# Where the norm factors of two-tile weight granules are applied, and on which engine their high parts are made

## The chip, the cores and the metric

The kernel runs on one core of one Trainium2 chip. The metric is the device time of one execution in microseconds (us). Engines are named as in the profile: PE is TensorE, DVE VectorE, ACT ScalarE, POOL GpSimd, SP the engine that issues the transfers (SPq its DMA queue). PEld is PE's loading of weights, which overlaps its matmuls.

## What is computed

A stack of four blocks over a sequence of 1024 positions, model width 1024, in float32. The first block (chunked gating and dilated attention) and the projections before the SSD are not touched. What the change meets, cut from the reference:

```python
def rmsnorm_2(x, g):
    return rms(x) * g

# mamba2_mixer: state-space scan (SSD) over chunks of 128, 4 groups
acum = cumsum(dt_k * Ag, axis=1)
decay = exp(where(causal, acum[:, None] - acum[None, :], -inf))
y = ssd_chunked_scan(xs, dt, A, Bm, Cm) + d_skip * xs
y = rms(y * silu(z), in 4 groups) * y_g          # y_g: 2048 factors
h = h + y @ w_out                                # m_out: 2048 x 1024

# per_layer_embedding, after each of the two mixers
h = h + (p_i @ w_proj) * sigmoid(rmsnorm_2(h, norm_g) @ w_gate)   # ple_gate: 1024 x 1024

# stick_breaking_mixer: 16 heads, causal, weights from suffix sums of log(1 - sigmoid)
h = h + (o * silu(gate)) @ w_out                 # s_out: 1024 x 1024
```

A norm's factors `g` are not multiplied into the activations: row k of the weight matrix is multiplied by `g[k]` when the weight is prepared.

## The kernel before, in words

**Parts.** Each float32 matmul is made of three products of a shorter format: a value is split into a high part (a rounded copy) and a low part (the value minus the high part), and PE adds high x high, high x low and low x high. So each weight passes through a preparation before PE can use it.

**Granules.** Class `Weights` (lines 366 to 427) prepares weights in granules of up to 1024 columns per partition. `loads` issues a DMA into a raw slot (names `m0f`, `m208f`; up to three slots of 4 KB per partition). `splits` takes a split slot (`m8r`, `m16r`, `m24r`, `m192r`, `m200r`; later `m140r`) and makes the parts: with a norm factor, first a pass of POOL over the whole raw granule that multiplies by the factors (`Gtt`, line 508, `m0f<-m0f,cols`; `cols` holds the factors, a column for each k-tile); then the high part on ACT (`A`, line 485, `m8r<-m0f`), or on POOL where `hi_on_pool` is set (`Gts`, line 512); then the low part on POOL (`Gtt`, line 508, `m8r<-m0f,m8r`). After this the raw slot is free for the next load. A granule holds 8 k-tiles of 128 columns (kind "b") or 2 k-tiles of 512 (kinds "a" and "c"). Of the second kind with a factor there are 32: 16 of `m_out` (gain `ynorm`) and 8 in each of the two `ple_gate` matrices.

**Order.** Every engine runs its instructions in an order that is fixed when the program is written out. Class `Sched` (lines 245 to 306) sets it: streams (Python generators with a priority) yield what they wait for, an estimate of engine times says when that is ready, and whenever PE's estimated time comes to a stream whose wait is over, the one of the best priority goes on. A stream may have a slack: it then goes on that much later than its wait says (`SLACK` is 1200 ns). So a cost or a wait that changes in one place can change the order of everything behind it.

**Stages**, in the order of time: first block to about 1250 us; `mamba` (projections of z, x, B, C and dt; a depthwise convolution; the SSD); `mamba_out` (`m_out`, from some 1930 us on, whose first half starts while the SSD's last group still runs); the first `ple`; `stick` (attention, 2300 to 2950 us; `W.limit(2, 1)` leaves two split slots and one raw slot, and `hi_on_pool` is set in its gate at the last head pair); `stick_out` (`s_out` in two blocks `so0` and `so1`, then the second `ple`).

*In `mamba`* `ev` starts the stream `tables` when the last piece of dt is there (line 1577). It makes the cumulative sums `acum` (PE: `psum<-m172f 32x128` and `128x256`), stores and reloads them, and makes the decay tables (DVE: `m172f<-m172f,m92f 128x128`, 8, and `m92f<-m92f 128x128`, 16). On DVE it shares the order with the taps of the convolution (`m60f`, `m76f`, `m44f`), from which come the B and C of the SSD's first product (PE: `psum<-m76f,m60f`). The SSD itself uses `m92f` (a table loaded from `acum`), `m172f` and `m192f` on DVE and POOL.

*In `stick_out`* the stream `more` (lines 2155 to 2157) waits until all scores are done (`all_scored`) and gives six split slots; three raw slots (`W.all_raw`) come back after `so1`. `load_halves` and its `one` load pairs `stk` and `sgd`, multiply them on POOL and split the product (POOL, then DVE) into the `so` matmuls' left operand (`m92r`, the last of them). `embed` loads `p` through `m172f`.

Helpers: all ACT operations of this kind have line 485, DVE 489 to 500 (500 is the operation with two tensors and a scalar), POOL 508 (two tensors) and 512 (one), DMA 516, matmuls 523, transposes 534.

## Time and profile before

| | us |
|---|---|
| median of 3 runs | 3232.16 |
| fastest and slowest of them | 3229.4, 3235.44 |
| the profiled execution | 3230.68 |
| its span in the trace | 3228.9 |
| PE busy | 3065.7 (95% of the span) |
| DVE busy | 1670.1 (52%) |
| ACT busy | 1386.8 (43%) |
| POOL busy | 1268.7 (39%) |

The span runs from the first to the last instruction of the trace; the execution's time has 1.8 us more around it. Busy shares are means over stages with different limits. A wait of PE is put down to the instruction whose result came last. The granted clock (PEclk) is a fraction of PE's full 2.4 GHz; 0.50 is 1.2 GHz.

### The profile page before, as it was taken

Reading aid. Unit: us, or ns where it says so; the run is one execution under the profiler, and the core shown is the slowest. Engines: PE = TensorE matmul, PEld = TensorE weight load, DVE = VectorE, ACT = ScalarE, POOL = GpSimd, SP = SyncE. Lnnn points to the kernel's source line nnn. Section 1 sums busy time; section 2 is a strip of 40 time slices with the busy share of each in tenths; the row PEclk is TensorE's granted clock in tenths of the full one; section 3 lists DMA queues with packets and bytes.
Section 4 is the critical chain, followed back from the end, with each engine's and each line's share of the span. In section 5 each row is a group of like instructions: output and inputs, shape, how many; then the busy total and the mean of one; then the engine's idle time right before and its main releaser. Section 6 shows DMA issues by size and latency. Waiting matters only on the chain. (4 is left out here: it accounts for less than half of the span.)

```text
span 3228.9 us, 40412 instructions
## 1 busy us (share of the span) xinstructions
PE 3065.7 (95%) x15374; PEld 2556.2 (79%) x15374; DVE 1670.1 (52%) x2944; ACT 1386.8 (43%) x2465; POOL 1268.7 (39%) x772
## 2 busy tenths in 40 slices
PE   8999999999999999999999999899999999988989
PEld 6888888888888788887777777678887777876777
DVE  2111146666674421557576765432457777777542
ACT  4322155556564311433243323222457776765321
POOL 3233111111111432324464554552445565657551
PEclk9999999999999999999999999999999999999999
DMA  4112221121122853332333444450301111113521
GB/s 142 55 65 73 91 64 52 59 67 53 55 63 76 276 172 137 110 90 66 100 102 102 102 117 140 147 189 27 101 12 34 46 34 39 40 40 114 206 89 52
DMA packets 270549, 290.85 MB, mean 90 GB/s; under 512 B 14660, under 2 KB 202228, under 8 KB 270356
## 3 DMA queue, kind: packets, MB, share of 16 engines
q1 hardware_dynamic: 270356, 288.29, 28.7%
q8 instruction: 120, 1.97, 0.3%
q14 instruction: 73, 0.60, 0.1%
HBM read 216.80 MB, written 71.43 MB: 89 GB/s over the span
## 5 line engine op out<-in xcount | busy, mean ns | idle before, releaser
L489 DVE TENSOR_TENSOR m156r<-psum,m156r 128x384 fp32r<-128x384 f32 (+2 forms) x376 | 223.4, 605 | 146.7 <-ACT m156r L485 144.7
L485 ACT ACTIVATE m156r<-psum 128x384 fp32r<-128x384 f32 (+2 forms) x376 | 194.6, 533 | 202.8 <-PE psum L534 191.0
L508 POOL TENSOR_TENSOR m172f<-m172f,m24f 128x127 f32<-128x127 f32 (+7 forms) x128 | 188.4, 1483 | 143.5 <-DVE m24f L2045 103.7
L508 POOL TENSOR_TENSOR m8r<-m0f,m8r 128x1024 fp32r<-128x1024 f32 x46 | 112.8, 2451 | 295.1 <-ACT m8r L485 290.3
L508 POOL TENSOR_TENSOR m16r<-m0f,m16r 128x1024 fp32r<-128x1024 f32 (+1 forms) x47 | 119.9, 2551 | 271.7 <-ACT m16r L485 221.6
L534 PE MATMUL psum<-ident,m172f 128*128 128x128 f32 (+1 forms) x1314 | 206.2, 281 | 19.6 <-POOL m172f L508 7.6
L2045 DVE TENSOR_TENSOR_SCAN m24f<-m24f,zero 128x128 f32<-128x128 f32 (+7 forms) x128 | 206.8, 1630 | 7.1 <-ACT m24f L485 6.7
L485 ACT ACTIVATE m192f<-psum 64x256 f32<-64x256 f32 (+2 forms) x231 | 102.8, 446 | 243.6 <-PE psum L523 136.3
L534 PEld LDWEIGHTS psum<-ident,m172f 128*128 128x128 f32 (+1 forms) x1314 | 158.9, 144 | 45.6 <-POOL m172f L508 10.2
L508 POOL TENSOR_TENSOR smalls<-smalls,mhalf 128x1 f32<-128x1 f32 (+1 forms) x104 | 91.0, 875 | 218.5 <-DVE smalls L496 217.9
L523 PE MATMUL psum<-m200r,m108r 128*128 128x512 f32 (+1 forms) x480 | 150.1, 393 | 6.5 <-POOL m200r L508 3.3
L508 POOL TENSOR_TENSOR m24r<-m0f,m24r 128x1024 fp32r<-128x1024 f32 (+1 forms) x40 | 100.9, 2524 | 135.5 <-ACT m24r L485 135.1
L523 PE MATMUL psum<-m108r 128*128 128x512 f32 (+3 forms) x384 | 142.8, 374 | 3.1 <-DVE smalls L1414 1.6
L494 DVE TENSOR_SCALAR m172f<-m172f,smalls 128x512 f32<-128x512 f32 (+7 forms) x160 | 130.5, 816 | 27.4 <-POOL smalls L508 22.8
L500 DVE SCALAR_TENSOR_TENSOR m172f<-m172f,psum 128x512 f32<-128x512 f32 x64 | 43.7, 686 | 188.2 <-ACT m172f L485 144.1
L1414 DVE CUSTOM_DVE_ANT_0 m172f<-psum,m24f 128x512 f32<-128x512 f32 (+1 forms) x192 | 102.8, 553 | 65.1 <-PE psum L523 64.9
L1422 ACT ACTIVATE m172f<-m172f,smalls 128x128 f32<-128x128 f32 (+7 forms) x128 | 99.4, 776 | 82.8 <-DVE smalls L496 81.2
L523 PE MATMUL psum<-m44r,m8r 128*128 128x512 f32 x504 | 133.8, 400 | 1.1 <-DVE m108r L500 1.1
L523 PE MATMUL psum<-m76r,m8r 128*128 128x512 f32 x504 | 132.7, 397 | 0.0
L523 PE MATMUL psum<-m60r,m8r 128*128 128x512 f32 x504 | 132.6, 397 | 0.0
L523 PE MATMUL psum<-m44r,m16r 128*128 128x512 f32 x492 | 132.4, 406 | 0.0
L523 PE MATMUL psum<-m60r,m16r 128*128 128x512 f32 x492 | 130.5, 398 | 0.0
(413 smaller groups left out, 7758.8 us busy)
## 6 DMA issues: line engine op xcount, KB each, us to landing
m0f<-in_w_in_dram SPq DMA_DIRECT2D x48, 512.0 KB, 3.8
m0f<-in_m_in_dram SPq DMA_DIRECT2D x26, 512.0 KB, 4.0
m208f<-in_w_in_dram SPq DMA_DIRECT2D x24, 512.0 KB, 4.1
m92f<-acum SPq DMA_DIRECT2D x21, 512.0 KB, 9.1
m24f<-in_alibi_dram SPq DMA_DIRECT2D x16, 512.0 KB, 4.2
m172f<-zd SPq DMA_DIRECT2D x32, 256.0 KB, 10.1
yd<-m172f SPq DMA_DIRECT2D x32, 256.0 KB, 2.6
m108f<-hd SPq DMA_DIRECT2D x16, 512.0 KB, 5.9
```

The source lines that it names most:

```text
L485: self.nc.scalar.activation(out, in_, func, **k)
L489: self.nc.vector.tensor_tensor(out, a, b, op=op)
L494: self.nc.vector.tensor_scalar(out, a, s1, None, op0=op0)
L500: self.nc.vector.scalar_tensor_tensor(out, a, s, b, op0=op0, op1=op1)
L508: self.nc.gpsimd.tensor_tensor(out, a, b, op=op)
L523: self.nc.tensor.matmul(out, l, r, start=start, stop=stop)
L534: self.nc.tensor.transpose(out, in_, self.ident[:in_.shape[0], :in_.shape[0]])
L1414: nc.vector.tensor_tensor_reduce(row[:, k0:k0 + w], bank[:, :w], Tt[:, off + k0:off + k0 + w], 1.0, -3e38, op0=ALU.add, op1=ALU.max, accum ...
L1422: nc.scalar.activation(row[:, :n], row[:, :n], AF.Exp, bias=nm, accum_out=l)
L2045: nc.vector.tensor_tensor_scan(x[:, ::-1], x[:, ::-1], self.zero.to_broadcast([P, n]), 1.0, op0=ALU.mult, op1=ALU.add)
```

## The change

Granules with a factor and at most two k-tiles take a new branch of `splits`. Each k-tile's high part is made by ACT straight from the raw granule, with the factor column as the activation's scale; each low part by one operation of DVE, raw x factor - high part. POOL has no part in them, and the raw slot is free after the last DVE operation. Stream `tables` gets a slack of four times `SLACK`. Stream `more` also ends `hi_on_pool` and gives the three raw slots back, at `all_scored`; the line that gave them back after `so1` goes.

```diff
--- before.py
+++ after.py
@@ -403,6 +403,19 @@
             hi = g.out[:, :n].rearrange("p (k c) -> p k c", k=g.nk)
             lo = g.out[:, KB4:KB4 + n].rearrange("p (k c) -> p k c", k=g.nk)
             dep = g.loaded.t
+            if g.gain is not None and g.nk <= 2:
+
+                yield (dep, b.s.FA)
+                for k in range(g.nk):
+                    e = b.A(R(hi[:, k, :]), g.rawv[:, k, :], AF.Copy, dep, scale=g.gain[:, k:k + 1])
+                for k in range(g.nk):
+                    yield (e, b.s.FV)
+                    t = b.Vstt(R(lo[:, k, :]), g.rawv[:, k, :], g.gain[:, k:k + 1], hi[:, k, :], ALU.mult, ALU.subtract, e)
+                self.raw.put(g.slot, t)
+                g.hi, g.lo = R(hi), R(lo)
+                g.ready.t = t
+                yield 0.0
+                continue
             if g.gain is not None:
                 yield b.s.FG
                 dep = b.Gtt(g.rawv, g.rawv, g.gain.unsqueeze(2).to_broadcast([P, g.nk, g.nc]), ALU.mult, dep)
@@ -1574,7 +1587,7 @@
                 if ps.free_size() > n:
                     r = self.Vtt(dtx[:, t * 32:t * 32 + 32], ps[:, 256:], kc[:, 0:32], ALU.add, max(e, ke))
                     if t == NT - 1:
-                        s.spawn(1, tables(r))
+                        s.spawn(1, tables(r), 4 * SLACK)
                 e = self.A(o, ps[:, :n], AF.Tanh, e, scale=0.5)
                 e = self.Vstt(o, o, 1.0, ps[:, :n], ALU.add, ALU.mult, e)
                 s.spawn(4, store(cb, t, o, e))
@@ -2154,6 +2167,8 @@
 
         def more():
             yield self.all_scored
+            self.hi_on_pool = False
+            W.raw.slots = W.all_raw
             W.split.slots = W.all[:4] + [self.region(o, 8, "r") for o in (140, 148)]
 
         s.spawn(1, more())
@@ -2188,7 +2203,6 @@
 
         yield from self.gemm_a(act, self.J["so", 1], ev, fin, 4, begin, (5, 6, 7))
         W.split.slots = W.split.slots + W.all[4:]
-        W.raw.slots = W.all_raw
 
         def store(t, e):
             yield e
```

Three places in the order of the engines follow. Line numbers of the changed kernel are 11 to 14 higher, so its helpers stand at L498 (ACT), L502 to L513 (DVE), L521 and L525 (POOL), L529 (DMA), L536 and L547 (PE).

PE at the tables of `mamba`, where `m108r`, `m140r` and `m156r` are the normed activations, `m8r` and `m200r` the weights of a projection, and `m172f` the operand of the cumulative sums. Before:

```order
L523 MATMUL psum<-m156r,m8r 128x512 x12
L523 MATMUL psum<-m108r,m200r 128x512 x3
L523 MATMUL psum<-m172f 32x128 x8
L523 MATMUL psum<-m172f 128x256 x2
L523 MATMUL psum<-m108r,m200r 128x512 x9
L523 MATMUL psum<-m140r,m200r 128x512 x12
```

and now:

```order
L536 MATMUL psum<-m156r,m8r 128x512 x6
L536 MATMUL psum<-m172f 32x128 x8
L536 MATMUL psum<-m172f 128x256 x2
L536 MATMUL psum<-m156r,m8r 128x512 x6
L536 MATMUL psum<-m108r,m200r 128x512 x12
L536 MATMUL psum<-m140r,m200r 128x512 x12
```

The cumulative sums stand 9 matmuls sooner.

POOL where the first granules of `m_out` are prepared, among the SSD's operations (`m92f`, `m172f`, `m192f`, and `m208f<-m208f,cols`, which is a granule again). Before:

```order
L508 TENSOR_TENSOR m0f<-m0f,cols 128x1024
L508 TENSOR_TENSOR m92f<-m92f,m192f 128x1024
L508 TENSOR_TENSOR smalls<-smalls,mhalf 128x1
L508 TENSOR_TENSOR m200r<-m0f,m200r 128x1024
L508 TENSOR_TENSOR m208f<-m208f,cols 128x1024
L508 TENSOR_TENSOR m172f<-m172f,m92f 128x512
L508 TENSOR_TENSOR m24r<-m208f,m24r 128x1024
L508 TENSOR_TENSOR m0f<-m0f,cols 128x1024
L508 TENSOR_TENSOR m192f<-m208f,m192f 128x512
L508 TENSOR_TENSOR m172f<-m172f 128x512
L508 TENSOR_TENSOR m172f<-m172f,m92f 128x512
L508 TENSOR_TENSOR m24r<-m0f,m24r 128x1024
```

and what DVE has there now (L513 with `cols` is the new form; `x2` is one granule; `m40f` belongs to the last convolution's inputs, `m44f` to its taps):

```order
L502 TENSOR_TENSOR m172f<-m172f 128x512
L513 SCALAR_TENSOR_TENSOR m40f<-m40f,psum 128x512
L507 TENSOR_SCALAR m172f<-m172f,smalls 128x512
L509 TENSOR_SCALAR smalls<-smalls 128x1
L513 SCALAR_TENSOR_TENSOR m200r<-m208f,cols,m200r 128x512 x2
L513 SCALAR_TENSOR_TENSOR m24r<-m0f,cols,m24r 128x512 x2
L507 TENSOR_SCALAR m172f<-m172f,smalls 128x512
L513 SCALAR_TENSOR_TENSOR m44f<-m92f,m192f,m44f 128x1023
L513 SCALAR_TENSOR_TENSOR m24r<-m208f,cols,m24r 128x512 x2
L513 SCALAR_TENSOR_TENSOR m44f<-m92f,m192f,m44f 128x1022
L513 SCALAR_TENSOR_TENSOR m16r<-m0f,cols,m16r 128x512 x2
```

The granules' two or three passes of POOL are gone from its queue, and their pairs stand in DVE's, among evacuations, the SSD's scales and the taps.

POOL in the last stage, where the granules of `ple_gate` in the second ple are prepared (`m140r`, `m24r`, `m200r`; `smalls` is the norm's power function). Before:

```order
L508 TENSOR_TENSOR m0f<-m0f,cols 128x1024
L512 TENSOR_SCALAR m140r<-m0f 128x1024
L508 TENSOR_TENSOR smalls<-smalls,mhalf 128x1
L508 TENSOR_TENSOR m140r<-m0f,m140r 128x1024
L508 TENSOR_TENSOR smalls<-smalls,mhalf 128x1
L508 TENSOR_TENSOR m0f<-m0f,cols 128x1024
L512 TENSOR_SCALAR m24r<-m0f 128x1024
L508 TENSOR_TENSOR m24r<-m0f,m24r 128x1024
L512 TENSOR_SCALAR m200r<-m208f 128x1024
L508 TENSOR_TENSOR smalls<-smalls,mhalf 128x1
L508 TENSOR_TENSOR m200r<-m208f,m200r 128x1024
L508 TENSOR_TENSOR m0f<-m0f,cols 128x1024
```

and the end of its queue now (`m40f`, `m0f`, `m192f` and `m92r` are pairs `stk` and `sgd` and their products; `m200r` is a granule of `ple_proj`, which has no factor):

```order
L521 TENSOR_TENSOR m192f<-m192f,m40f 128x512
L525 TENSOR_SCALAR m92r<-m192f 128x512
L521 TENSOR_TENSOR m40f<-m40f,m0f 128x512
L525 TENSOR_SCALAR m92r<-m40f 128x512
L521 TENSOR_TENSOR smalls<-smalls,mhalf 128x1 x7
L521 TENSOR_TENSOR m200r<-m208f,m200r 128x1024
L521 TENSOR_TENSOR smalls<-smalls,mhalf 128x1
```

The passes of the granules with factors are gone; only the low part of `ple_proj` is left. In the same place SP issued, before,

```order
L516 DMA m0f<-in_s_out_dram 128x2x512
L516 DMA m0f<-stk 128x512
L516 DMA m40f<-sgd 128x512
L516 DMA m172f<-hq 128x1024
L516 DMA m172f<-in_p_dram 128x256
L516 DMA m172f<-hq 128x1024
L516 DMA m172f<-in_p_dram 128x256 x3
L516 DMA m0f<-in_ple_proj_dram 128x2x512
```

and now

```order
L529 DMA m192f<-sgd 128x512
L529 DMA m192f<-stk 128x512
L529 DMA m40f<-sgd 128x512
L529 DMA m172f<-hq 128x1024 x2
L529 DMA m172f<-in_p_dram 128x256 x4
L529 DMA m40f<-stk 128x512
L529 DMA m0f<-sgd 128x512
L529 DMA m172f<-hq 128x1024 x2
L529 DMA m0f<-in_ple_gate_dram 128x2x512
```

The last pair `stk`, `sgd` stood behind four loads of `p` and stands behind eight.

## Rows read from the trace of the kernel before

**Rows 1.** Stages: us, busy us (instructions) of PE, PEld, DVE, ACT, POOL; PEclk; DMA share; GB/s.
```profile
1930.00:2110.00 180.00, 157.54 (x782) 125.02 (x781) 90.67 (x142) 57.37 (x95) 94.60 (x64) 0.95 0.49 145
2300.00:2950.00 650.00, 611.60 (x3324) 517.93 (x3323) 454.89 (x657) 436.55 (x823) 371.44 (x213) 0.98 0.14 42
```

**Rows 2.** TensorE's waits, 2000 to 2300 us: us in total, times, longest.
```profile
PE psum L523 <- DVE m192f L489: 4.3, 1, 4.3
PE psum L523 <- POOL m200r L508: 4.0, 2, 3.3
PE psum L523 <- ACT m200r L485: 3.2, 1, 3.2
PE psum L523 <- POOL m172f L508: 2.1, 1, 2.1
```

**Rows 3.** GpSimd's timeline, 2018 to 2045 us: start, us, what [idle before <-releaser].
```profile
2032.10 1.89 POOL L508 TENSOR_TENSOR m0f<-m0f,cols 128x1024 f32<-128x1024 f32 x1
...
2036.17 1.04 POOL L508 TENSOR_TENSOR m172f<-m172f,m92f 128x512 f32<-128x512 f32 x1
```

**Rows 4.** VectorE's timeline, 2018 to 2050 us.
```profile
2024.31 2.56 DVE L494 TENSOR_SCALAR m172f<-m172f,smalls 128x512 f32<-128x512 f32 x1 [1.55 <-POOL smalls L508]
...
2042.07 1.66 DVE L496 TENSOR_SCALAR m92f<-m92f 128x128 f32<-128x128 f32 x8 [7.90 <-DMA m92f<-acum]
```

**Rows 5.** TensorE's timeline, and a row of the table of stages.
```profile
2045.46 3.55 PE L523 MATMUL psum<-m24r,m140r 128*128 128x512 f32 x6
...
2044.00:2049.00 5.00, 4.63 (x9) 3.02 (x10) 3.30 (x7) 2.37 (x4) 3.17 (x3) 0.50 0.28 106
```

**Rows 6.** TensorE's waits, 3061 to 3125 us.
```profile
PE psum L523 <- POOL m24r L512: 5.6, 1, 5.6
PE psum L523 <- POOL m24r L508: 1.6, 1, 1.6
PE psum L523 <- DVE m92r L500: 1.1, 1, 1.1
PE psum L523 <- POOL m140r L508: 1.0, 1, 1.0
```

**Rows 7.** GpSimd's timeline, 3070 to 3123 us.
```profile
3112.67 1.89 POOL L508 TENSOR_TENSOR m0f<-m0f,cols 128x1024 f32<-128x1024 f32 x1 [3.48 <-DMA m0f<-in_ple_gate_dram]
3114.65 1.05 POOL L512 TENSOR_SCALAR m24r<-m0f 128x1024 fp32r<-128x1024 f32 x1
```

**Rows 8.** Groups by shape of three engines: count, busy us, mean ns; idle before, releasers.
```profile
L508 POOL TENSOR_TENSOR m0f<-m0f,cols 128x1024 f32<-128x1024 f32 x53 | 105.4, 1988 | 31.1 <-DMA m0f<-in_ple_gate_dram 18.0 <-DMA m0f<-in_s_in_dram 8.6 <-DMA m0f<-in_m_out_dram 4.5
L508 POOL TENSOR_TENSOR m24r<-m0f,m24r 128x1024 fp32r<-128x1024 f32 x39 | 97.9, 2511 | 135.5 <-ACT m24r L485 135.1
...
L485 ACT ACTIVATE m172f<-psum,rq 128x512 f32<-128x512 f32 x96 | 66.6, 694 | 0.0
...
L485 ACT ACTIVATE m8r<-m0f 128x1024 fp32r<-128x1024 f32 x43 | 45.5, 1058 | 26.5 <-POOL m0f L508 8.4 <-PE psum L523 7.0 <-issue 5.4
...
L500 DVE SCALAR_TENSOR_TENSOR m156f<-psum,cols,m172f 128x512 f32<-128x512 f32 x16 | 12.0, 751 | 157.2 <-PE psum L523 157.2
...
L500 DVE SCALAR_TENSOR_TENSOR m108r<-m172f,m108r 128x512 fp32r<-128x512 f32 x8 | 5.5, 693 | 26.9 <-ACT m108r L485 26.9
```

**Rows 9.** GpSimd's timeline, 1440 to 1475 us.
```profile
1454.73 3.40 POOL L508 TENSOR_TENSOR m92f<-m92f,m192f 128x1024 f32<-128x1024 f32 x1
```

**Rows 10.** TensorE's timeline around the tables, then VectorE's.
```profile
1417.02 5.32 PE L523 MATMUL psum<-m172f 128*32 128x128 f32 x20 [5.41 <-issue]
...
1426.98 2.88 PE L523 MATMUL psum<-m108r,m200r 128*128 128x512 f32 x12
...
1434.91 5.43 DVE L496 TENSOR_SCALAR m92f<-m92f 128x128 f32<-128x128 f32 x16
```

**Rows 11.** SP's DMA queue, 3030 to 3080 us: issues.
```profile
3057.79 0.33 SPq L516 DMA_DIRECT2D m40f<-sgd  x1
...
3062.68 1.73 SPq L516 DMA_DIRECT2D m172f<-in_p_dram  x3
```

## Prediction

> **What bounds the kernel now.** I read the table of stages first, then TensorE's waits in two stretches, then the timelines of GpSimd and VectorE there. TensorE is the engine that is nearly always busy: even in the stretch from 1930 to 2110 us, where the SSD ends and `m_out` starts, it works 157.5 of 180 us, while GpSimd is busy 94.6 and VectorE 90.7 [rows 1]. So only what makes TensorE stand still, or run at the lower clock, is worth anything, and the question is which of its waits come from the granules that the change touches.
>
> There are two such places. **The start of m_out:** TensorE stands 3.2 us for the high part (ACT) and 3.3 us for the low part (GpSimd) of one granule, `m200r`, 2.1 us for GpSimd's `m172f` and 4.3 us for `m192f`, 12.9 us in all; a further 0.7 us for another `m200r` (4.0 in two waits, the longer 3.3) lies in the first ple [rows 2]. GpSimd is the common cause: the SSD's product of 2036.17 us stands in its queue behind granule passes, the nearest a gain pass of 1.89 us at 2032.10 [rows 3]. That product is the last to read `m92f`; only then can the next `acum` table be loaded there, and VectorE stands 7.90 us for this load until 2042.07 [rows 4], so that `m192f` reaches TensorE late. VectorE is held up by GpSimd directly as well: a 128x512 scale took 2.56 us [rows 4], as long as one of GpSimd's low parts (2.51 in the mean) [rows 8]. After these waits the granted clock is 0.50, that is 1.2 of 2.4 GHz: six matmuls take 3.55 us [rows 5] where twelve take 2.88 at the higher level [rows 10].
>
> **The tail:** for `ple_gate` of the second ple TensorE stands 5.6 us for a high part of GpSimd, 1.6 us for its low part and 1.0 us for the granule before, 8.2 us in all [rows 6]. One raw slot is in use. A load starts when the low part before has ended (3.48 us of idle time), then come the gain pass (1.89), the high part (1.05) and the low part (2.4): about 10 us a granule [rows 7], while TensorE comes to all four granules of a column block within its first row tile, 24 matmuls.
>
> **The change, part by part.** *The granules.* 32 granules (16 of `m_out`, 2x8 of `ple_gate`) lose a gain pass of 1.99 us and a low part of 2.51 us on GpSimd and a copy of 1.06 us on ACT (high part, or 1.05 us on GpSimd in the tail) [rows 7, 8]. GpSimd gives up 32 x 4.5 = 144 us. Each gets two ACT copies of 128x512 with a pointer scale, at 0.69 us each by the row with such a scale, and two VectorE operations of 128x512 with two SBUF inputs and a pointer. Their nearest row is the 0.75 us of the form with a pointer (its one input in PSUM) [rows 8]. ACT gains some 0.3 us a granule, VectorE 64 x 0.75 = 48 us. From landed load to both parts it was 1.99 + 1.06 + 2.51 = 5.6 us in a queue with other work; it is now the two copies, and a last VectorE operation behind them, 1.4 + 0.75, or 3 us with the handovers. This new form runs nowhere before. Its lower bound is 0.69 us; its upper bound is a wait behind a GpSimd pass of 2.5 us.
>
> *m_out.* A split slot is released in the last row tile of one column block and used in the first of the next, 24 matmuls later, which is 5.5 us or more at the higher clock. Three us of conversion fit into that, 5.6 us behind other work on GpSimd did not: I take the two `m200r` waits as gone (-6.5). Of the two SSD waits (6.4) the GpSimd queue in front of them falls, but the load of `acum` stays: half (-3.2). Of the matmuls at half clock here (3.55 against 1.5 us in the one row, about 5 us over the stretch) I take half (-2.5). The new VectorE pairs stand in its order ahead of the SSD's scale and of the transposes' evacuations: +2. Together **-10**, between -18 (all of it, nothing given back) and -2. *First ple*: -0.7, from -0.7 to 0.
>
> The contention between VectorE and GpSimd speaks against the new form. Rows first: a GpSimd product, 2.55 us in the mean of its form, took 3.40 us at 1454.73 us while VectorE ran taps with two SBUF inputs [rows 9]; the 64 new operations can hold GpSimd up by their own 48 us at most, while the 144 us of passes that held VectorE up are gone. The sum goes by these rows: no further charge. The Trainium skill, page "SBUF — State Buffer", section "Who interferes with whom", says that a VectorE instruction with two SBUF inputs contends with a GpSimd instruction that reads SBUF, and that whoever issues first blocks the other entirely; the rows agree with that. By that rule alone the removed passes and the added operations nearly cancel where they alternate, and m_out would keep its SSD waits.
>
> *The tables* (slack). In the order TensorE's cumulative sums stand 9 matmuls sooner, at 0.24 us each, but their operand from VectorE is not earlier: the wait of 5.41 us grows by 2.2. The first product of C and B stands a further 9 matmuls sooner, while on VectorE the end of the taps is now behind the 8 + 16 decay scales (5.43 us for 16) [rows 10]; 0 to 2.8 us more. Part of it can be earned back, since what follows starts earlier. **+2**, from 0 to +5.
>
> *The stick stage* only changes its order. TensorE is idle there for 650 - 611.6 = 38.4 us in many small waits [rows 1]. No instruction goes; GpSimd still splits the granules of the first `s_out` block itself. **+1**, from -6 to +8, a sixth to a fifth of that idle time in either direction.
>
> *The tail.* With three raw slots from `all_scored` on, a granule is loaded before its turn, and its parts need 3 us of ACT and VectorE in place of the chain of 10. The last of them takes a slot of the second `s_out` block and is used 24 matmuls and 12 transposes later, some 6.5 us. The 8.2 us go, and about 2 us of matmuls at half clock behind them; a little stays as VectorE serves evacuations too: **-9.5**, from -12 to -2. The four granules of the second `s_out` block and two of `ple_proj` only move their high part to ACT; it is covered by the block before.
>
> Sum: +2 - 10 - 0.7 + 1 - 9.5 = -17.2 us. The profiled execution took 3230.7 us (span 3228.9), 1.5 us under the median of 3232.2: 3213.5 for that execution, **3215** against the median.
>
> **The rivals.**
> *A, the tail gives it back one step earlier.* The last k-panel of the second `s_out` block, `m92r`, needs a pair of loads, a GpSimd product, and a split; TensorE waits 1.1 us for it now [rows 6]. In the new order of SP's queue the last pair stands behind the second batch of `p` loads, which wait for slots: these went out at 3062.68 to 3064.4, the pair's last load at 3057.79 [rows 11]. Up to 6.6 us later, plus a few matmuls less of cover: about 8 us of new wait, 3223. For it: the order. Against it: the pair's slot comes free earlier, as GpSimd no longer has the granules between. 0.14.
>
> *B, m_out gives nothing.* The SSD is bound by the `acum` load and VectorE, and the granule waits only become waits for those: 3225 to 3227. For it: 7.90 us of waiting for that load [rows 4]. Against it: the load starts only after GpSimd's product. 0.12.
>
> *C, slower.* The pairs on VectorE stand between the SSD's steps, each behind two ACT copies: a granule can block VectorE for 1.4 + 1.5 = 2.9 us, 24 granules (16 of `m_out`, 8 of the first ple) for 70 us. Once more than 17 + 6.5 = 24 us of that lie on TensorE's path the kernel is slower by over 0.2%; at 27 us it is 3242. For it: VectorE is half busy in that stretch already, and TensorE waits for it there [rows 1, 2]. Against it: the other half is idle, and 2.5 us blocks by GpSimd disappear. 0.08.
>
> *D, nothing measurable.* The two gains are made up by the reordered stick stage and the tables: 3230. 0.06.
>
> **How the numbers follow.** The forecast has 0.60, with 3205 to 3224 as its own range. About 0.2% (6.5 us) is what a measurement of this kernel can tell from no change, so faster means under 3225.7: the forecast, nearly all of A and a third of B, 0.77; the rest of A, B and D within, 0.15; C slower, 0.08. The range 3203 to 3229 leaves out C, most of D and the forecast's low end, under 2 in 10.
>
> **What would show it.** In the profile after: GpSimd busy some 140 us less; no wait of TensorE for `m200r` or `m24r` from GpSimd, neither near 2020 nor near 3115 us; the new VectorE form at 0.7 to 0.8 us; the wait near 1417 us at 7.6 us. Wrong would be a wait for `m92r` above 5 us, a new wait for VectorE's granules (`m24r`, `m16r`) in m_out, or over 45 us idle in the stick stage.

## The result and the profile after

The changed kernel takes 3187.4 us (median of 4 runs, 3183.3 to 3192.3) against 3231.0 for the kernel before on the same chip (median of 4, 3229.4 to 3235.4): 0.9864 of its time, 95% interval 0.9843 to 0.9884. That is 43.6 us, where 17 were forecast; it lies below the range that was given. The profiled execution is the slowest of the four, 3192.3 us with a span of 3190.6.

The totals of the page, PE, PEld, DVE, ACT, POOL:

```profile
PE 3066.8 (96%) x15374; PEld 2557.1 (80%) x15374; DVE 1694.9 (53%) x3008; ACT 1410.7 (44%) x2511; POOL 1104.3 (35%) x694
```

TensorE's work is the same (3066.8 us busy against 3065.7), GpSimd has 164 us less, VectorE 25 and ACT 24 more. The table of stages (us; busy us and instructions of PE, PEld, DVE, ACT, POOL; granted clock; DMA share; GB/s):

```profile
1930.00:2110.00 180.00, 169.88 (x849) 136.44 (x848) 96.48 (x172) 63.37 (x111) 46.54 (x42) 0.98 0.55 179
2300.00:2950.00 650.00, 616.01 (x3311) 518.25 (x3309) 473.82 (x666) 443.09 (x835) 390.34 (x233) 0.96 0.16 48
3061.00:3125.00 64.00, 64.00 (x308) 53.27 (x307) 24.90 (x43) 21.46 (x37) 6.07 (x7) 1.00 0.08 25
```

The first row stands against the first of [rows 1]: in the same 180 us TensorE works 169.9 us instead of 157.5, GpSimd 46.5 instead of 94.6, the granted clock is 0.98 instead of 0.95. In the stretch of the last ple, where it stood 9.3 us before [rows 6], TensorE now has no gap at all. The middle row looks like nothing: 616.0 against 611.6 us busy. It is a different piece of work, though, since the stage now begins earlier, and this is where most of the forecast's error lies.

**The same work, side by side.** To compare stages whose order differs I added up TensorE's matmuls through each trace, each at the time that its shape takes at the higher clock, and looked up when either kernel reaches the same sum. Section 1 runs from 1364 us of the kernel before (the last projections, the tables, most of the SSD), 2 from 1990 (rest of the SSD, `m_out`, first ple), 3 from 2273 (the end of the first ple, stick, both `s_out` blocks), 4 from 3075 to the start of the last matmul (last ple). The lower rows say how much of a section TensorE stood idle; the rest is matmul time.

| us | 1 | 2 | 3 | 4 |
|---|---|---|---|---|
| before | 625.8 | 283.1 | 801.7 | 148.0 |
| changed | 627.8 | 265.4 | 790.9 | 137.0 |
| saved | -2.0 | 17.7 | 10.8 | 11.0 |
| forecast | -2 | 10.7 | -1 | 9.5 |
| idle before | 35.2 | 18.9 | 59.4 | 8.2 |
| idle changed | 32.0 | 6.2 | 45.3 | 0.0 |

TensorE's waits from 2000 to 2300 us, which answer to [rows 2] (us in total, times, longest):

```profile
PE psum L536 <- DVE m172f L502: 2.8, 2, 2.5
PE psum L547 <- DVE m60r L502: 1.7, 1, 1.7
PE psum L547 <- DVE m108f L502: 1.5, 1, 1.5
```

All four of those rows are gone; 6.0 us remain, for other things. The 2.8 us for `m172f` are new: four of the new operations stood before it on VectorE, which had first waited for the `acum` load (VectorE's timeline, then TensorE's wait):

```profile
2018.94 1.66 DVE L509 TENSOR_SCALAR m92f<-m92f 128x128 f32<-128x128 f32 x8 [7.17 <-DMA m92f<-acum]
2020.51 2.07 DVE L513 SCALAR_TENSOR_TENSOR m24r<-m0f,cols,m24r 128x512 fp32r<-128x512 f32 x3
...
2023.10 0.75 DVE L513 SCALAR_TENSOR_TENSOR m24r<-m0f,cols,m24r 128x512 fp32r<-128x512 f32 x1
2023.76 0.69 DVE L502 TENSOR_TENSOR m172f<-m172f,psum 128x512 f32<-128x512 f32 x1
...
2024.51 0.49 PE L536 MATMUL psum<-m76f 128*128 128x128 f32 x2 [2.46 <-DVE m172f L502]
```

At the tables, against 5.41 us [rows 10]:

```profile
PE psum L536 <- issue: 5.8, 1, 5.8
PE psum L536 <- DVE m76f L513: 1.6, 1, 1.6
```

and from 2950 us to the end:

```profile
PE psum L536 <- POOL m76r L525: 2.9, 1, 2.9
PE psum L536 <- POOL m16r L521: 2.8, 1, 2.8
PE psum L536 <- POOL m8r L521: 1.9, 1, 1.9
...
PE psum L536 <- DVE m92r L513: 0.4, 1, 0.4
```

No granule of `ple_gate` is waited for, and `m92r`, rival A's place, costs 0.4 us. New is `m76r`, 2.9 us for another of the pairs. The new operations, VectorE's and then ACT's (count, busy us, mean ns; idle before and its releaser):

```profile
L513 DVE SCALAR_TENSOR_TENSOR m24r<-m0f,cols,m24r 128x512 fp32r<-128x512 f32 x14 | 9.9, 747 | 3.6 <-ACT m24r L498 3.6
...
L513 DVE SCALAR_TENSOR_TENSOR m192r<-m208f,cols,m192r 128x512 fp32r<-128x512 f32 x2 | 3.5, 1788 | 0.0
```

```profile
L498 ACT ACTIVATE m24r<-m0f,cols 128x512 fp32r<-128x512 f32 x14 | 9.5, 720 | 8.2 <-DMA m0f<-in_m_out_dram 4.2 <-PE psum L536 3.5 <-DMA m0f<-in_ple_gate_dram 0.5
```

VectorE's form takes 0.75 us where GpSimd is not in its way: so did the 54 of the 64 that no GpSimd operation overlapped. In the worst of the groups, one granule at 2136 us, its two operations took 1.79 us in the mean. Line numbers are each kernel's own.

### The profile page after: what moved, and what is told of

Its sections match the earlier page's. It is cut to its first block, busy times and chain, and to the rows that moved or that the text cites. A ratio compares the mean times of both kernels' runs of the same rounds, so it can differ in the third digit from the quotient of the medians.

```text
span 3190.6 us, 40526 instructions
## 1 busy us (share of the span) xinstructions
PE 3066.8 (96%) x15374; PEld 2557.1 (80%) x15374; DVE 1694.9 (53%) x3008; ACT 1410.7 (44%) x2511; POOL 1104.3 (35%) x694
## 5 line engine op out<-in xcount | busy, mean ns | idle before, releaser
L502 DVE TENSOR_TENSOR m156r<-psum,m156r 128x384 fp32r<-128x384 f32 (+2 forms) x376 | 223.9, 605 | 147.6 <-ACT m156r L498 145.3
L498 ACT ACTIVATE m156r<-psum 128x384 fp32r<-128x384 f32 (+2 forms) x376 | 196.7, 535 | 185.6 <-PE psum L547 176.4
L521 POOL TENSOR_TENSOR m172f<-m172f,m24f 128x127 f32<-128x127 f32 (+7 forms) x128 | 181.0, 1424 | 156.2 <-DVE m24f L2058 108.2
L2058 DVE TENSOR_TENSOR_SCAN m24f<-m24f,zero 128x128 f32<-128x128 f32 (+7 forms) x128 | 219.4, 1722 | 6.5 <-ACT m24f L498 5.5
L547 PE MATMUL psum<-ident,m172f 128*128 128x128 f32 (+1 forms) x1314 | 206.5, 281 | 15.5 <-DVE m172f L507 7.2
L521 POOL TENSOR_TENSOR m16r<-m0f,m16r 128x1024 fp32r<-128x1024 f32 (+1 forms) x44 | 107.9, 2452 | 301.1 <-ACT m16r L498 250.3
L498 ACT ACTIVATE m192f<-psum 64x256 f32<-64x256 f32 (+2 forms) x230 | 102.1, 445 | 239.7 <-PE psum L536 137.7
L521 POOL TENSOR_TENSOR m8r<-m0f,m8r 128x1024 fp32r<-128x1024 f32 x42 | 102.7, 2445 | 274.9 <-ACT m8r L498 237.1
L547 PEld LDWEIGHTS psum<-ident,m172f 128*128 128x128 f32 (+1 forms) x1314 | 158.9, 144 | 43.8 <-DVE m172f L507 9.0
L521 POOL TENSOR_TENSOR smalls<-smalls,mhalf 128x1 f32<-128x1 f32 (+1 forms) x104 | 92.1, 886 | 278.4 <-DVE smalls L509 277.7
L536 PE MATMUL psum<-m108r 128*128 128x512 f32 (+3 forms) x384 | 143.2, 375 | 13.0 <-ACT m172f L498 11.3
L536 PE MATMUL psum<-m200r,m108r 128*128 128x512 f32 (+1 forms) x480 | 151.0, 395 | 0.0
L513 DVE SCALAR_TENSOR_TENSOR m172f<-m172f,psum 128x512 f32<-128x512 f32 x64 | 43.7, 686 | 188.9 <-ACT m172f L498 144.1
L536 PE MATMUL psum<-m44r,m8r 128*128 128x512 f32 x504 | 134.6, 405 | 1.1 <-DVE m108r L513 1.1
L507 DVE TENSOR_SCALAR m172f<-m172f,smalls 128x512 f32<-128x512 f32 (+7 forms) x160 | 122.6, 766 | 24.3 <-POOL smalls L521 19.8
L536 PE MATMUL psum<-m60r,m8r 128*128 128x512 f32 x504 | 133.3, 398 | 0.3
L536 PE MATMUL psum<-m76r,m8r 128*128 128x512 f32 x504 | 132.3, 397 | 0.0
L536 PE MATMUL psum<-m60r,m16r 128*128 128x512 f32 x492 | 132.2, 399 | 0.0
L536 PE MATMUL psum<-m92r,m8r 128*128 128x512 f32 x504 | 130.7, 395 | 0.0
L536 PE MATMUL psum<-m44r,m16r 128*128 128x512 f32 x492 | 130.6, 402 | 0.0
```

Of the source, the lines that this page charges most:

```text
L498: self.nc.scalar.activation(out, in_, func, **k)
L502: self.nc.vector.tensor_tensor(out, a, b, op=op)
L507: self.nc.vector.tensor_scalar(out, a, s1, None, op0=op0)
L513: self.nc.vector.scalar_tensor_tensor(out, a, s, b, op0=op0, op1=op1)
L521: self.nc.gpsimd.tensor_tensor(out, a, b, op=op)
L536: self.nc.tensor.matmul(out, l, r, start=start, stop=stop)
```

## The experiments

Ratios are to the kernel before on the same chip, with the 95% interval. The kernel before ran at 3236 to 3239 us in these comparisons. The table has the four sections of each run's profiled execution, counted as above, then TensorE's idle time in section 3 and the time of one piece of section 3, from 2850 to 2943 us of the kernel before. Runs with the order of the kernel before in section 3 are marked with * (e3 and e8 leave it at its end, where their flags act).

| run | ratio | 1 | 2 | 3 | 4 | idle in 3 | 2850-2943 |
|---|---|---|---|---|---|---|---|
| before | | 625.8 | 283.1 | 801.7* | 148.0 | 59.4 | 93.1 |
| changed | 0.9864 | 627.8 | 265.4 | 790.9 | 137.0 | 45.3 | 84.1 |
| e1_granules | 0.9858 | 627.2 | 265.7 | 784.0 | 142.4 | 44.3 | 84.3 |
| e2_tables | 0.9944 | 632.2 | 284.2 | 784.1 | 144.8 | 45.0 | 84.2 |
| e3_tail | 0.9990 | 630.8 | 283.6 | 810.0* | 141.0 | 63.7 | 93.1 |
| e4_granules_tail | 0.9857 | 627.2 | 267.3 | 788.1 | 137.0 | 45.4 | 84.2 |
| s_before_shift | 0.9977 | 628.7 | 286.4 | 790.5 | 148.6 | 51.3 | 84.0 |
| s_before_shift2 | 0.9952 | 631.6 | 284.0 | 791.8 | 146.8 | 51.4 | 85.8 |
| s_after_shift | 0.9871 | 640.1 | 264.8 | 799.4 | 137.0 | 54.4 | 91.3 |
| s_after_shift2 | 0.9885 | 631.3 | 267.9 | 797.8 | 137.0 | 49.8 | 87.1 |
| e5_mo_only | 0.9867 | 630.9 | 266.4 | 788.8 | 137.8 | 47.4 | 84.0 |
| e6_pool_passes | 0.9915 | 627.9 | 270.4 | 792.8 | 140.7 | 47.3 | 84.3 |
| e7_last_ple_only | 0.9967 | 629.3 | 283.6 | 802.7* | 140.7 | 60.4 | 92.8 |
| e8_last_ple_slots | 0.9974 | 625.5 | 283.8 | 804.9* | 140.7 | 61.6 | 92.9 |

The theories at the start. *Order:* the 10.8 us of section 3 come from the other order in which the stick stage is written out, which any shift of the estimated times brings. *Flags:* they come from `hi_on_pool` and the raw slots at `all_scored`.

### The change in its three parts

**e1_granules**, the new branch of `splits` alone:

```diff
@@ splits @@
+            if g.gain is not None and g.nk <= 2:
...
+                continue
             if g.gain is not None:
```

> Only the new branch of the granules; tables without slack, hi_on_pool and the raw slots as before. The changed kernel saved some 17.7 us by the end of the first ple, 10.8 us from there through the second s_out block, 11 us in the last ple (work done by TensorE against time, profiled executions). Order theory (the 10.8 us come from another written-out order of the stick stage, which any shift of the estimate brings): 17 to 19 us saved by the end of the first ple, the stick stage anywhere from -6 to +10, the tail 7 to 11 (one raw slot, so each load still shows): 3191 to 3212 us. Flag theory (the 10.8 us come from hi_on_pool and the raw slots at all_scored): stick and s_out give nothing, 3202 to 3207 us.

Measured 3191.2 us, 0.9858 (0.9839 to 0.9877): as fast as the whole change, at the fast end of the order theory's span and, by the ratio, beyond it. Section 3 is 784.0 without any flag, which the flag theory excludes; it gains 17.7, which is also more than the 10 that the order theory gave the stick stage at most.

**e2_tables**, the slack alone:

```diff
-                        s.spawn(1, tables(r))
+                        s.spawn(1, tables(r), 4 * SLACK)
```

> Only the slack of the tables. Local cost as predicted: +2 us by 1900 us (0 to +5), the m_out waits unchanged. Order theory: the stick stage moves by up to 8 us in either direction although nothing in it is changed: 3225 to 3241 us. Flag theory: within 3 us of before plus the local cost, 3230 to 3236 us.

Measured 3217.6 us, 0.9944 (0.9926 to 0.9961): 18 us faster, though nothing is removed and the tables themselves wait longer. Sections 1 and 2 lose 7.5 us together, section 3 gains 17.6, more than the order theory allowed. Where the order matters can be seen at the end of a head pair. TensorE's timeline of the kernel before (start, us, instructions; in brackets the idle time and its releaser):

```profile
2859.22 1.63 PE L523 MATMUL psum<-m92r,m16r 128*128 128x512 f32 x6
...
2867.89 1.22 PE L523 MATMUL psum<-m156r 128*128 128x256 f32 x4 [3.46 <-DVE m192f L489]
...
2872.28 1.75 PE L523 MATMUL psum<-m156r 128*128 128x256 f32 x7 [1.47 <-DVE m156r L489]
...
2876.51 0.85 PE L523 MATMUL psum<-m44r,m8r 128*128 128x512 f32 x3
```

and the same piece of work in this run:

```profile
2865.20 0.86 PE L523 MATMUL psum<-m92r,m16r 128*128 128x512 f32 x3
...
2866.15 0.95 PE L523 MATMUL psum<-m92r,m16r 128*128 128x512 f32 x3
...
2868.54 0.50 PE L523 MATMUL psum<-m108r 128*128 128x512 f32 x1 [1.09 <-ACT m172f L485]
...
2870.21 0.57 PE L523 MATMUL psum<-m156r 128*128 128x256 f32 x3 [0.83 <-DVE m156r L489]
...
2872.51 1.48 PE L523 MATMUL psum<-m44r,m8r 128*128 128x512 f32 x3
```

`m92r,m16r` and `m44r,m8r` are dense projection matmuls; `m156r` and `m108r` the attention's weighted sums and scores, which need an operation of ACT and one of VectorE for each. Before, the last dense matmuls are issued at 2859.22, and after them the attention's pieces follow one another, several waiting for an evacuation, 3.46 us the longest; the next dense matmuls come at 2876.51. In the run the dense matmuls stretch to 2866.15 and the next projection's begin at 2872.51, with waits of about 1 us. The waits cost a second time through the clock. Two stretches of the kernel before:

```profile
2860.00:2880.00 20.00, 14.36 (x70) 12.26 (x69) 14.56 (x22) 16.19 (x33) 6.33 (x5) 0.74 0.16 47
2952.00:2972.00 20.00, 10.37 (x41) 7.90 (x41) 14.32 (x18) 7.79 (x16) 19.74 (x16) 0.66 0.56 183
```

and of the run, at about the same work:

```profile
2861.00:2881.00 20.00, 18.09 (x89) 14.50 (x89) 16.14 (x25) 16.25 (x30) 6.58 (x6) 0.91 0.20 59
...
2945.00:2965.00 20.00, 12.53 (x50) 9.19 (x50) 18.18 (x21) 8.08 (x16) 19.13 (x17) 0.74 0.62 195
```

Before, the granted clock averages 0.74 over the 20 us there and 0.66 over 20 us a head pair later; in the run it is 0.91 and 0.74. Over the whole of section 3 the idle time is the larger part: 45.0 us instead of 59.4, which is 14 of the 17.6 us.

**e3_tail**, the flags alone:

```diff
             yield self.all_scored
+            self.hi_on_pool = False
+            W.raw.slots = W.all_raw
...
-        W.raw.slots = W.all_raw
```

> Only hi_on_pool ended and the three raw slots given back at all_scored; order the same as before until there. Order theory: the tail saves 4 to 10 us (loads hidden, the gain passes and low parts still on GpSimd), s_out 0 to 3: 3218 to 3228 us. Flag theory: 10.8 us in s_out besides: 3208 to 3217 us.

Measured 3234.7 us, 0.9990 (0.9980 to 1.0001): no difference that can be told, and slower than either theory had it. Section 4 gains 7.0 and section 3 loses 8.3, of which 4.5 lie behind 2943 us of the kernel before; the order ahead of the flags is unaltered, so the rest is the difference between two executions. TensorE's waits from 3050 to 3110 us:

```profile
PE psum L534 <- DVE m156r L489: 3.3, 1, 3.3
PE psum L534 <- DVE m108f L489: 2.3, 1, 2.3
PE psum L523 <- DVE m92r L500: 2.2, 1, 2.2
```

VectorE's timeline there, and GpSimd's:

```profile
3062.76 2.38 DVE L500 SCALAR_TENSOR_TENSOR m92r<-m192f,m92r 128x512 fp32r<-128x512 f32 x1
...
3068.20 3.82 DVE L489 TENSOR_TENSOR m108f<-m108f,m172f 128x1024 f32<-128x1024 f32 x2
```

```profile
3062.69 1.90 POOL L508 TENSOR_TENSOR m0f<-m0f,cols 128x1024 f32<-128x1024 f32 x1
...
3068.12 1.27 POOL L508 TENSOR_TENSOR m40f<-m40f,m192f 128x512 f32<-128x512 f32 x1
3069.48 1.47 POOL L512 TENSOR_SCALAR m92r<-m40f 128x512 fp32r<-128x512 f32 x1
```

The gain passes are still on GpSimd, but now they run while the last pairs are split: VectorE's `m92r` low part took 2.38 us beside the pass of 3062.69 (0.69 is usual for the shape [rows 8]), and two additions 3.82 us beside a product and a split of pairs (2.35 in the changed kernel at 2109 us, with no GpSimd operation beside them). TensorE got rid of the waits for granules and waits for `m156r`, `m108f` and `m92r` instead, 7.8 us. The 5.5 us for `m156r` and `m92r`, where the kernel before has 1.7, are at rival A's place, by another mechanism; the 2.3 for `m108f` come later, in the last ple.

**e4_granules_tail**, the branch and the flags, without the slack:

```diff
-                        s.spawn(1, tables(r), 4 * SLACK)
+                        s.spawn(1, tables(r))
```

(against the changed kernel)

> The change without the slack of the tables. Order theory: 28 us for certain (17.7 + 11, tables +1 to +2 better), the stick stage anywhere from -6 to +10: 3191 to 3209 us. Flag theory: the same as the changed kernel less the tables, 3183 to 3191 us.

Measured 3190.5 us, 0.9857 (0.9840 to 0.9875), the same as the whole change and as e1. So beside the branch neither the slack nor the flags show in the time (the flags do in section 4: 137.0 against 142.4 in e1). The three parts do not add up: by the ratios they give 46, 18 and 3 us alone and 44 together, since the branch and the slack both leave the slow order of section 3 (93.1 us to some 84 in the last column), and that can be left only once.

### Order alone

Four kernels move the planner's estimate on where the stick stage begins. No instruction is added, removed or altered, and the order before that place stays.

```diff
     def stick(self):
+        self.s.now += 1200.0
+        for k in self.s.e:
+            self.s.e[k] += 1200.0
```

**s_before_shift**, the kernel before, 1200 ns:

> The kernel before, its estimate of the time of all engines moved on by 1.2 us where the stick stage begins; no instruction added, removed or changed, everything before that place in the same order. The end of its stick stage then stands in an order much like the changed kernel's (seven rows in ten of TensorE's list agree; with the kernel before it is half). Order theory: 10 to 18 us faster than before, all of it between the start of the stick stage and the second s_out block: 3215 to 3225 us if before is at 3232. Rival (the stick stage gains because something is removed or freed): within 3 us of before.

Measured 0.9977 (0.9968 to 0.9987), 3228.0 us: 7.5 us by the ratio, under the 10 to 18 of the total; section 3 gains 11.2, as the theory says, and sections 1 and 2, whose order is not altered, were 6 us longer in the profiled execution.

**s_before_shift2**, the kernel before, 1800 ns:

> The kernel before, its estimate moved on by 1.8 us at the start of the stick stage; an order that resembles neither the kernel before's (four rows in ten) nor the changed one's. Order theory: the time differs from before by anything between -20 and +8 us, 5 us or more being likely, all between the start of the stick stage and the end; rival: within 3 us.

Measured 0.9952 (0.9935 to 0.9969), 3224.5 us: some 15 us faster, section 3 at 791.8.

**s_after_shift**, the changed kernel, 2400 ns:

> The changed kernel with the same estimate moved on by 2.4 us at the start of the stick stage; its stick stage then ends in an order much like the kernel before's (seven rows in ten). Order theory: the 10 to 15 us of the stick stage are lost again, m_out and tail stay: 3195 to 3205 us. Rival: within 3 us of the changed kernel, 3184 to 3192 us.

Measured 3195.5 us (3193.0 to 3211.9), 0.9871 (0.9855 to 0.9888). Its interval overlaps with the changed kernel's, so by the total it decides nothing. In the profiled execution section 3 is 799.4, 8.5 us of the changed kernel's 10.8 lost again; but that execution was the slowest of its five, by 15 us. The piece from 2850 to 2943 is 91.3 there, nearly that of the kernel before.

**s_after_shift2**, the changed kernel, 600 ns:

> The changed kernel, its estimate moved on by 0.6 us at the start of the stick stage; order again unlike both. Order theory: -5 to +12 us against the changed kernel (3185 to 3200 us if before is at 3232), since the changed kernel's own order is one of the better ones so far; rival: within 3 us.

Measured 3203.5 us (3199.2 to 3205.1), 0.9885 (0.9867 to 0.9903): about 7 us more than the changed kernel by the two ratios, whose intervals overlap; section 3 at 797.8.

Taken together: with the order of the kernel before, section 3 took 801.7, 802.7 and 804.9 us (810.0 where the flags collide in it); in ten other runs 784.0 to 799.4. Those ten are some seven orders, as the changed kernel, e1, e4 and e5 have nearly the same one (12 to 106 of its 3955 matmuls stand elsewhere); between these four section 3 still varied by 6.9 us, so one execution places an order only roughly. The idle time is steadier: 44.3 to 47.4 us in those four, 59.4 to 63.7 with the order of the kernel before, 45.0 to 54.4 in the other six. Three of the ten came to the kernel before with nothing of the granules changed, and all three were faster by ratios whose intervals stay clear of 1. The kernel before has the slowest order seen; the changed kernel's lies in the middle of the rest. Most of the difference is the piece from 2850 to 2943 us: 92.8 to 93.1 with the order of the kernel before, 84.0 to 87.1 in nine of the ten, and 91.3 in the one whose section 3 is the slowest of them.

### m_out and the last ple

**e5_mo_only**, the branch for `m_out` alone (against the changed kernel):

```diff
-            if g.gain is not None and g.nk <= 2:
+            if getattr(g, "direct", False):
...
+            for gs in J["mo", kh].blocks:
+                for g in gs:
+                    g.direct = True
```

> The changed kernel with the new branch for the 16 granules of m_out alone; the ple_gate granules (16) go through GpSimd's gain pass and low part again, with the high part on ACT and three raw slots in the last ple. Theory: m_out's 17 to 20 us stay, the 0.7 to 3 us of the first ple go, and of the 11 us of the tail about half stays (loads hidden, 5.5 us of passes a granule against 6.5 of cover): 3188 to 3196 us. Rival (the raw slots alone cure the tail): as the changed kernel. Other rival (GpSimd's passes are the whole of the tail): the tail waits 8 to 11 us as before, 3194 to 3203 us.

Measured 3192.7 us, 0.9867 (0.9852 to 0.9882). Section 2 keeps 16.7 of 17.7 us, and section 4 is 137.8, within 1 us of the changed kernel, though its granules go through GpSimd's passes. With the loads ahead of time those passes are covered, as the first rival had it; the theory left half of the tail's gain.

**e6_pool_passes**, the changed kernel with GpSimd's occupancy put back. The extra products write a tile that nobody reads:

```diff
+                b.s.spawn(0, b.passes(dep))
                 yield (dep, b.s.FA)
...
+    def passes(self, dep):
+        for n in range(2):
+            yield (dep, self.s.FG)
+            for _ in range(3):
+                i = self.ident.unsqueeze(1).to_broadcast([P, 2, P])
+                self.Gtt(self.junk.rearrange("p (a b) -> p a b", a=2), i, i, ALU.mult, dep)
```

> The changed kernel with six extra GpSimd products of 128x256 for each of the 32 granules (a constant times itself into a tile that nobody reads, some 4 us), so that GpSimd is as busy as before but no granule waits for it. Occupancy theory (m_out gained because the SSD's GpSimd products no longer stand behind granule passes): by the end of the first ple 6 to 12 us of the 17 to 20 are lost, with TensorE waiting for m172f and m192f again. Latency theory (it gained because the granules themselves are ready sooner): at most 3 us lost there. The tail stays within 3 us in either case. The stick stage may move by up to 15 us with its order, so the verdict is read from the place, not from the total.

Measured 3207.6 us, 0.9915 (0.9898 to 0.9931), 16 us over the changed kernel by the ratios. In the stretch from 1930 to 2110 us GpSimd is busier than in the kernel before (114.3 us against 94.6 [rows 1]); the table of stages and TensorE's waits there:

```profile
1930.00:2110.00 180.00, 167.49 (x825) 134.57 (x824) 108.94 (x166) 58.99 (x104) 114.34 (x131) 0.97 0.52 167
```

```profile
PE psum L557 <- DMA m44f<-yd: 5.7, 1, 5.7
PE psum L546 <- DVE m192f L504: 3.4, 1, 3.4
...
PE psum L546 <- POOL m172f L523: 0.8, 1, 0.8
```

Of the two SSD waits `m192f` is back (3.4 us) and `m172f` nearly not (0.8); section 2 loses 5.0 of its 17.7 us, just under the 6 that occupancy gave and over the 3 that latency allowed. So more than a quarter of m_out's gain is put down to GpSimd's free queue. That the larger part is the granules' own shorter way is what is left over, not shown: the order of section 2 is another one here too. Section 4 loses 3.7 us, where at most 3 were expected.

**e7_last_ple_only**, the kernel before with the branch for the last `ple_gate` alone, the order unaltered until the last `s_out` weights:

```diff
+            if getattr(g, "direct", False):
...
+            for gs in self.J["pg", i, cb].blocks:
+                for g in gs:
+                    g.direct = i == 1
```

> The kernel before with the new branch for the 8 ple_gate granules of the last ple alone; one raw slot, high parts of the others on GpSimd, the same order until the last weights of s_out. Tail theory (GpSimd's passes make the 8.2 us of waits there and 2 us of half clock): those waits go and the kernel is 8 to 11 us faster. Rival (the tail's gain in the changed kernel also hangs on its other order, as the tables' slack alone took 5 us off the same waits): 2 to 6 us faster.

Measured 0.9967 (0.9952 to 0.9981), 3228.1 us: some 10 us faster; section 4 gains 7.3. TensorE's waits from 3060 us on:

```profile
PE psum L547 <- DVE m44r L502: 1.8, 2, 1.1
PE psum L547 <- DVE m92r L502: 1.1, 1, 1.1
PE psum L536 <- DVE m92r L513: 1.1, 1, 1.1
```

None is for a granule. One raw slot is enough for the granules when the passes are short; e1, with one slot too, has 4.0 us of waits in the last ple, none for a granule either.

**e8_last_ple_slots**, the same with the flags of e3:

> The same, and the flags at all_scored: three raw slots, high parts on ACT. Tail theory: as the run above, within 2 us, since either alone takes the waits of the last ple away. Rival (the earlier loads and passes collide with the last k-panel of s_out, as in the run of the flags alone, where waits for m156r, m92r and m108f of 2 to 3 us each came instead): 3 to 6 us slower than the run above.

Measured 0.9974 (0.9962 to 0.9985), 3230.3 us: not to be told from e7, and section 4 is 140.7 in both. So either the branch or the slots takes the waits for granules out of the last ple, and here having both adds nothing that shows. A wait of e3's kind comes even so, once: TensorE stood 4.5 us for `m156r`, as a new pair of 2.69 us and two additions stood ahead of it on VectorE:

```profile
3057.45 2.69 DVE L513 SCALAR_TENSOR_TENSOR m16r<-m0f,cols,m16r 128x512 fp32r<-128x512 f32 x2
...
3062.80 0.69 PE L547 MATMUL psum<-ident,m172f 128*128 128x128 f32 x2 [4.45 <-DVE m156r L502]
```

No version was run that beats the changed kernel: the ratios of e1, e4 and e5 lie within its interval.

## Why the prediction was wrong

**The step that failed: the stick stage "only changes its order", +1, from -6 to +8.** Section 3 gave 10.8 us back instead. The step held that a new order is as likely to lose as to gain, and bounded it by a sixth to a fifth of the idle time that TensorE had there, 38.4 us [rows 1]; no row gave that fraction. Over the same matmul work, kernel before first, then the changed one:

```profile
2300.00:2943.00 643.00, 604.60 (x3281) 511.79 (x3280) 450.13 (x649) 432.12 (x813) 367.45 (x209) 0.98 0.13 40
...
2282.20:2915.60 633.40, 608.09 (x3277) 512.81 (x3276) 452.89 (x646) 430.58 (x810) 361.31 (x209) 0.97 0.14 41
```

TensorE stood idle 643.0 - 604.6 = 38.4 us before and 633.4 - 608.1 = 25.3 now. So 13.1 us of idle time went, a third of it and not a sixth; 3.5 us came back as longer matmul time, as the granted clock was 0.97 instead of 0.98. The stage is 9.6 us shorter (6.1 if it is cut at 2950 us, where the orders differ); the other 1.2 lie in the end of the first ple, and the `s_out` blocks gave nothing. Some 9 us are the piece from 2850 to 2943 us, whose idle time fell from 8.1 to 2.1 us; there the matmuls gained 2.9 us as well, at a granted clock of 0.98 instead of 0.94. And the kernel before was no middle of a spread: all ten other runs were faster in this section, by 2.3 to 17.7 us. The prediction read nothing from the new order of this stage, so it was luck that the term came out as a gain. Rival D, which had the stick stage take the gains away, erred to the same side.

**m_out and the first ple: -10.7, measured -17.7.** The mechanism was right and the size off, within the bound of -18 that was given. The same section of the kernel before and of the changed one:

```profile
1990.00:2273.00 283.00, 264.06 (x1247) 214.43 (x1246) 101.41 (x167) 76.01 (x126) 130.09 (x82) 0.97 0.37 120
...
1991.20:2256.60 265.40, 259.16 (x1246) 211.50 (x1245) 124.44 (x222) 84.67 (x147) 59.21 (x50) 0.99 0.42 136
```

The `m200r` waits went as forecast, 7.2 us. The two waits of the SSD, of which half was counted (3.2), went whole, 6.4; half of the matmuls at half clock was counted (2.5), and the matmul time fell by 4.9. Two waits of the transposes for VectorE's evacuations were not in the sum. The kernel before had these of them from 2000 to 2300 us:

```profile
PE psum L534 <- DVE m44r L489: 4.5, 3, 1.8
...
PE psum L534 <- DVE m108f L489: 0.9, 1, 0.9
```

That is 5.4 us, and 3.2 are left (`m60r`, `m108f`, above). The 2 us given back for VectorE's fuller queue came, as the 2.8 us for `m172f` behind the new operations. Together 7.2 + 6.4 + 4.9 + 2.2 - 2.8 = 17.9.

**The tail: -9.5, measured -11.0**, right in size: 8.2 us of idle time, and 2.7 of matmul time at half clock where 2 were taken. The reason given, three raw slots and short parts, was more than was needed: e5 and e7 show that either is enough to end the waits for granules.

**The tables: +2, measured +2 by the waits.** 5.8 + 1.6 = 7.4 us of waiting in place of 5.4; every run with the slack has 7.3 to 8.4, every run without it 5.4. The split was off: the first wait grew by 0.4, not 2.2, and the second product waits 1.6 us, inside the 0 to 2.8. That section 1 as a whole also lost 2.0 is luck: it contains some 2.4 us of gain at the start of m_out, from 1930 us on, and executions of one order differ by 6 us there.

**Prices.** VectorE's new form 0.75 us, as taken; 64 of them 52.7 us instead of 48, as a few stand behind a GpSimd operation. VectorE's total rose by only 25, so its other operations, as many as before, took 28 us less; that this was time lost beside GpSimd's passes is argued, not shown. ACT's 0.72 instead of 0.69. GpSimd 164 us less instead of 144: the high parts of the tail (14 of about 1.1 us) were left out of that term.

**The rivals.** B did not come (section 2 gained more than forecast): VectorE still waits 7.17 us for the `acum` load, but TensorE no longer for `m192f`. Nor did C, beyond the 2.8 us for `m172f`: no wait for a VectorE granule in m_out. A did not come in the changed kernel; its wait is 0.4 us. Something like its exchange of waits happened in e3, 5.5 us in place of 1.7. The VectorE-GpSimd contention, which was weighed and not charged, shows in e3 and in the form's 1.79 us, and cost the changed kernel 4.7 us of VectorE time; it did not keep the SSD's waits, which fell from 6.4 to 2.8 us.

**What stays open.** The profiled sections add up to 37.5 us where the medians differ by 43.6; the profiled execution is the slowest of four (two lie at 3183.5, two at 3191 to 3192, with mean granted clocks of 0.983 and of 0.978 to 0.979, and what makes the two levels was not tried). Which feature of an order makes the piece from 2850 to 2943 us slow was seen, in the place of the dense matmuls, and not tested. In m_out the share of GpSimd's queue rests on one run, with passes of another shape than those removed and with another order.

## What to carry to other kernels

Where a planner writes the order of the instructions, every edit is two edits: what it does, and the new order behind it. Before you credit a part with a gain, shift the planner's estimate with nothing else changed and see how far the time moves; here that was 7.5 and 15 us, a sixth and a third of the whole change. Then compare stages over the same matmul work, TensorE's idle time and its matmul time apart: here the idle time told the orders of section 3 from one another more clearly than its length did. A fraction of the idle time is no bound for a reorder unless something gives the fraction: here a third of it went. And where TensorE's waits stand close together (0.74 of the clock over 20 us), the matmuls between them cost time as well, which a sum of idle time doesn't contain.

## What the runs showed of the hardware that was not expected

The same instructions in the same order took 625.5 to 631.6 us over section 1 in six of the kernels above that share the order of the kernel before there, and 627.8 to 640.1 in those with the changed one's: up to 12 us of difference between executions. Between the two extremes, s_after_shift and the changed kernel, 7.9 us are matmul time, at a mean granted clock of 0.95 and 0.96, and 4.4 idle time. Over the whole span the mean granted clock went from 0.975 (3210.1 us, s_after_shift) to 0.983 (3182.0 us, another execution of the changed kernel).

VectorE's new form can take more than three times its 0.75 us. The slowest granule of the changed kernel, on VectorE with the operation before it, and on GpSimd:

```profile
2135.34 1.22 DVE L502 TENSOR_TENSOR m108f<-m108f,m172f 128x1024 f32<-128x1024 f32 x1
2136.53 3.50 DVE L513 SCALAR_TENSOR_TENSOR m192r<-m208f,cols,m192r 128x512 fp32r<-128x512 f32 x2
```

```profile
2135.97 2.86 POOL L521 TENSOR_TENSOR m16r<-m0f,m16r 128x1024 fp32r<-128x1024 f32 x1 [52.69 <-ACT m16r L498]
```

The granule's two operations, 1.4 us by themselves, took 3.50 us (2.84 the first), and started 0.6 us after a GpSimd low part that itself took 2.86 instead of some 2.4. Both lost time. The Trainium skill, page "SBUF — State Buffer", section "Who interferes with whom", says that VectorE's second input from SBUF comes through a port that it shares with GpSimd, that the shared ports are an exclusive lock, and that the order of issue decides who blocks. These rows agree with that on both sides: the GpSimd operation started 0.6 us before the end of a VectorE addition with two inputs in SBUF, and took some 0.46 us longer; the granule's first operation ended 0.5 us after the GpSimd operation did.
